# One PSUM tile for the grouped products, and score buffers of a bank and a half in the attention

## The chip, the cores and the metric

The kernel runs on one core of one Trainium2 chip. The metric is the device time of one execution in microseconds (us), the median of several runs. A core has a matrix engine (TensorE, PE in the profile, with its weight loads shown apart as PEld), a vector engine (VectorE, DVE), a scalar engine (ScalarE, ACT), a general engine (GpSimd, POOL) and a queue engine (SyncE, SP). Each takes its instructions in order. Matrix products land in PSUM, 128 partitions of eight banks; a bank holds 512 fp32 numbers of a partition. From there DVE or ACT read them.

## The reference, cut to what matters

One layer of a block with two parallel mixers over 512 latent tokens of width 2048. A combined projection gives queries, keys, values, gates and the input of a Fourier mixer. Twelve query heads share four key and value heads; the keys are the 512 tokens and 256 context tokens, so each block of 128 queries meets 768 keys:

```
s = jnp.einsum('bqhgd,bkhd->bhgqk', qi, k, preferred_element_type=jnp.float32)
w = jax.nn.softmax(s, axis=-1).astype(v.dtype)
return jnp.einsum('bhgqk,bkhd->bqhgd', w, v)
...
y_a = (attn * jax.nn.silu(z_a)) @ w_pa
y_b = (_fourier_mix(u_b) * jax.nn.silu(z_b)) @ w_pb
return (g_a * y_a + g_b * y_b) @ w_o
```

All is fp32. The kernel gets fp32 accuracy from three products of split operands.

## The kernel before, in words

**Split products.** `mm3` (lines 292 to 296) computes one product of two operands that are each held as a high and a low part: high by high (L294), high by low (L295) and low by high (L296). `split_from` (L161) makes the parts: ACT writes the high part (L162), then DVE writes the low part (L163).

**Stages.** First come the modulation and the start of the projection, with a PSUM pool of their own that is closed at L655. Then the groups of 1024 output columns (`KINDS`, L58: three of queries and gates "qz", two gates, one "kv", two gates), then the attention, then the projection of both branches, merged, and the output product as two more groups.

**Groups.** A group is computed by seven products of half-size blocks (`ONE_GROUP`, L52; a Strassen form), each of 48 matrix instructions. P1 and P2 sum up in the PSUM buffer "a", Q5, Q6 and Q3 in "b", P7 and Q4 in "c". "a" and "c" are pairs of banks under the name "x", "b" under the name "y". After each product the sum is taken out by ACT or DVE (L756 to L782); after Q4 the DVE subtraction of `sub` (L756) reads "c". `qz_done` (L849) takes further pairs as scratch for tanh and rotation. So a qz group takes three pairs of x: for P1, for P7, and for the tanh after P7.

**PSUM before.** From L662 on one pool `psp` holds two buffers of two banks under the tag x, and one each under y0 and y1. `pair("x")` asks the pool for the next x; the pool decides which of the two it is. `pair("y")` takes turns by hand.

**The attention** (L1109 to L1212) has 48 steps, one for each head and block of 128 queries. In a step, `scores` writes 768 scores into an x pair (matrix instructions of 512 and of 256 columns), DVE takes the maximum (L1118), ACT the exponential (L1120). A step later `turn` transposes the 768 probabilities on PE into `tp`, one of the y pairs (six instructions, L1136), and `split_from` makes them into high and low (`pth`, `ptl`). Every other step `values` multiplies them with the values in half of the other y pair (18 instructions of 256 columns) and transposes the gate (L1151). `turn_queries` transposes the next head's queries (L1017), `get_keys` the next keys (L1010). `filler` (L1076) puts products of the Fourier branch in between, into the other half of that y pair; ACT copies them out (L1096).

**Order.** The program is written in the order above, but a scheduler of the framework orders the instructions of each engine anew and sets the semaphores. It keeps two engines out of one PSUM bank: an instruction that writes a bank waits until the readers of that bank are done, also where they read other columns of it. What depends on what is kept per tile: a new tile of the pool waits for the whole old one. Weights come by DMA on SP's queue (L198, L201), sums of weights by accumulating DMA on POOL's (L250).

Of the kernel before, what the change touches and what calls it, by code (L numbers as in the profile page):

```python
# [10 lines left out]
F32 = mybir.dt.float32  # L11
# [7 lines left out]
P = 128  # L19
# [8 lines left out]
NKEY = T + C  # L28
# [79 lines left out]
def block_kernel(ctx, tc, xT, ctx_rows, ctx_toks, x, c_row, w_ss, w_gate, vecs, qkg, rope, dft_c, dft_s,  # L108
# [29 lines left out]
    def uid(s):  # L138
        cnt[0] += 1
        return f"{s}{cnt[0]}"  # L140
# [20 lines left out]
    def split_from(src, hi, lo):  # L161
        nc.scalar.activation(hi, src, ACT.Copy)  # L162
        return nc.vector.tensor_tensor(lo, src, hi.bitcast(F32), op=ALU.subtract)  # L163
# [92 lines left out]
    def get(key):  # L256
        load_more()
        turn = [e for e in ahead if not e.aside]
        assert turn[0].key == key, (turn[0].key, key)
        for e in turn[: len(hl_pools)]:  # L260
            split_piece(e)
        load_more()
        e = turn[0]
        ahead.remove(e)
        free.extend(p[0::2] for p, _ in e.raws if p in retired)
        return e.raws[0][1] if e.kind == "raw" else e.out
# [15 lines left out]
    def take(shape, dt=F32, pool=None):  # L282
        p = next((p for p in free if p[0] is pool), free[0])
        free.remove(p)
        t = slot_tile(p, shape, dt)
        home[id(t)] = p, t
        return t

    def give(*ts):
        free.extend(home.pop(id(t))[0] for t in ts)  # L290

    def mm3(o, ah, al, bh, bl, start, stop, cont=False):

        nc.tensor.matmul(o, ah, bh, start=start, stop=False, skip_group_check=cont)  # L294
        nc.tensor.matmul(o, ah, bl, start=False, stop=False, skip_group_check=cont)  # L295
        nc.tensor.matmul(o, al, bh, start=False, stop=stop, skip_group_check=cont)  # L296
# [34 lines left out]
    def tiles(key):  # L331

        new = [take((1024,), F32R) for _ in range(2)]
        kept.setdefault(key, []).extend(new)
        return new
# [15 lines left out]
    flat = lambda v: v.rearrange("p t c -> p (t c)")  # L351
# [14 lines left out]
    for g in range(LAST + 1):  # L366
        for name in ONE_GROUP:
            if (g, name) == (LAST, "Q4"):
                stream_keys(0)
            if g == KV:  # L370
                f = CTX_FORMS.index(next(f for n, f, _, _ in PRODUCTS if n == name))
# [288 lines left out]
    new_ev = lambda: evp.tile([P, 2, 512], F32, tag="ev", bufs=4, name=uid("ev"))  # L660
    qzs, qzp = region("qzp", "right", reuse_waits="tile")
    psp = ctx.enter_context(tc.tile_pool(name="psp", bufs=1, space=PSUM, reuse_waits="tile"))  # L662
    last_y = [0]
    rows4 = lambda hi, lo: [(hi[:, j, :], lo[:, j, :]) for j in range(4)]

    def make_form(f, h):
# [20 lines left out]
        return rows4(hi, lo)  # L687

    def pair(tag, skip=0):
        if tag == "y":  # L690
            last_y[0] += 1 + skip
            return psp.tile([P, 2, 512], F32, tag=f"y{last_y[0] % 2}", bufs=1, name=uid(tag))
        return psp.tile([P, 2, 512], F32, tag=tag, bufs=2, name=uid(tag))


    forms = {"A11": [(hhi[j][:, :256], hlo[j][:, :256]) for j in range(8)],
# [9 lines left out]
    class Banks:  # L706


        def __init__(self):
            self.b = [pair("x") for _ in range(2)]  # L710
# [4 lines left out]
    class Group:  # L715
# [12 lines left out]
        def run(self, name):  # L728
            form, which = next((f, c) for n, f, _, c in PRODUCTS if n == name)
            start = which not in self.acc  # L730
            if start:

                self.acc[which] = Banks() if self.last and which == "c" else pair(self.tags[which])
# [137 lines left out]
    class Context:  # L871
# [13 lines left out]
        def products(self, name, which, pc, w, start):  # L885
            a = self.acc[:, 1 if which == "b" else 0, :]
            for k in range(2):
                j = 2 * pc + k
                fh, fl = (f.parts[j // 4][:, j % 4 // 2, P * (j % 2) : P * (j % 2) + P] for f in self.f)
                mm3(a, fh, fl, w[0][:, k, :], w[1][:, k, :], start and pc == 0 and k == 0, pc == 3 and k == 1,  # L890
                    cont=not start)
# [23 lines left out]
        def values(self, b, v):  # L915
            nc.scalar.dma_start(by_group(v_d[:, :, 4 + b, :]), v.rearrange("p (g d) -> p g d", g=4))
# [60 lines left out]
    def load_row(half):  # L977
        row = crow[half] = take((1024,)) if half else rp.tile([P, 1024], F32, tag="raw1", bufs=1, name=uid("crow"))
        nc.gpsimd.dma_start(row, c_row[:, 1024 * half : 1024 * half + 1024].broadcast_to([P, 1024]))

    def silu_of_row(half):

        e, row = take((1024,)), crow[half]
        nc.scalar.activation(e, row, ACT.Tanh, scale=0.5)
        nc.vector.scalar_tensor_tensor(row, e, 1.0, row, op0=ALU.add, op1=ALU.mult)
        give(e)
# [15 lines left out]
    def load_head(h):  # L1002
        qz[h] = take((2, 4, HD))
        nc.gpsimd.dma_start(qz[h], qz_d[h])

    def get_keys(g):
        raw = get(("K", g))
        tk = flat(pair("x"))
        for t in range(KT):
            nc.tensor.transpose(tk[:, t * P : (t + 1) * P], raw[:, t * P : (t + 1) * P], ident)  # L1010
        keys = tiles(g)
        split_from(tk[:, :NKEY], *(w[:, :NKEY] for w in keys))
        kv[g] = tuple(keys) + get(("V", g))

    def turn_queries(h, tq):
        for t in range(4):
            nc.tensor.transpose(tq[:, t * P : (t + 1) * P], qz[h][:, 0, t, :], ident)  # L1017
        qs[h] = take((2, T), F32R)
        split_from(tq, qs[h][:, 0, :], qs[h][:, 1, :])
# [47 lines left out]
    free += [(hm, f"s{(9 + i) % KK}") for i in range(KK)]  # L1067
    ats_, atp = region("atp", "right", reuse_waits="tile")

    turned_y = last_y[0] % 2  # L1070
    both = pair("y")
    fill_acc, b1 = both[:, 0, :], lambda: both[:, 1, :]
    assert not any(p[0] is gvp or p[2] == "raw1" for e in ahead for p, _ in e.raws)
    ybs, S = {}, {}

# [26 lines left out]
    def fill(n):  # L1102
        for _ in range(n):
            next(fl, None)
# [4 lines left out]
    def scores(i):  # L1109
        h, t = divmod(i, 4)  # L1110
        kh, kl = kv[h // GQ][:2]
        s = slice(t * P, (t + 1) * P)
        qh, ql = qs[h][:, 0, s], qs[h][:, 1, s]
        sc = flat(pair("x"))
        for a, b in ((0, 512), (512, 768)):
            mm3(sc[:, a:b], qh, ql, kh[:, a:b], kl[:, a:b], True, True)
        mx = stats[:, 4 * (i % 4) : 4 * (i % 4) + 4]
        nc.vector.tensor_reduce(mx[:, 0:1], sc[:, :NKEY], axis=AX.X, op=ALU.max, negate=True)  # L1118
        probs[i] = take((NKEY,))
        nc.scalar.activation(probs[i], sc[:, :NKEY], ACT.Exp, bias=mx[:, 0:1], accum_out=mx[:, 1:2])  # L1120
        if t == 3:
            give(qs.pop(h))

    def divide(i):

        h, t = divmod(i, 4)
        z = qz[h][:, 1, t, :]
        r = stats[:, 4 * (i % 4) + 2 : 4 * (i % 4) + 3]
        nc.vector.reciprocal(r, stats[:, 4 * (i % 4) + 1 : 4 * (i % 4) + 2])
        nc.vector.tensor_scalar(z, z, r, None, op0=ALU.mult)  # L1130

    def turn(i):
        p = probs.pop(i)
        tp = flat(psp.tile([P, 2, 512], F32, tag=f"y{turned_y}", bufs=1, name=uid("tp")))
        for k in range(KT):
            nc.tensor.transpose(tp[:, k * P : (k + 1) * P], p[:, k * P : (k + 1) * P], ident)  # L1136
        if i % 2 == 0:
            pts[i // 2] = [atp.tile([P, KT, 256], F32R, tag=n, bufs=2, name=uid(n)) for n in ("pth", "ptl")]
        c = slice((i % 2) * P, (i % 2) * P + P)
        split_from(tp[:, :NKEY].rearrange("p (k q) -> p k q", k=KT), *(w[:, :, c] for w in pts[i // 2]))  # L1140
        give(p)
# [38 lines left out]
    for i in range(NSTEP + 3):  # L1180
        h, t = divmod(i, 4)
        if i < NSTEP:
            if t == 1 and h + 2 < NH:
                load_head(h + 2)
            if i == 24:
                load_row(0)
            elif i == 28:
                silu_of_row(0)
            if i % 12 == 10 and i // 12 + 1 < NKV:
                get_keys(i // 12 + 1)  # L1190
            scores(i)
        want = min(3 + 61 * (i + 1) // NSTEP, 64)
        if want > filled:
            fill(1)
            filled += 1
        if i % 2 == 0 and i >= 4:
            values((i - 4) // 2)
        if 1 <= i <= NSTEP:
            turn(i - 1)
            divide(i - 1)  # L1200
        if t == 1 and h + 1 < NH:
            turn_queries(h + 1, b1())
        if want > filled:
            fill(want - filled)
            filled = want
        if i == NSTEP - 1:
            fill(1)
            first_sums = [pair("x") for _ in range(2)]
            first = products(CHUNKS[0], first_sums)
        if NSTEP > i - 2 >= NSTEP - 3:  # L1210
            next(first)
            next(first)  # L1212
# [12 lines left out]
    m = -1  # L1225
# [46 lines left out]
    for n, j in enumerate(CHUNKS):  # L1272
# [9 lines left out]
        for pc, t in products(j, accs) if n else first:  # L1282
# [4 lines left out]
            if pc > 3:  # L1287
                y = ybs[j, pc - 4]
# [274 lines left out]
```

## Time and profile before

| | |
|---|---|
| median of 3 runs | 1337.47 us (1337.39 to 1337.62) |
| the profiled execution | 1337.45 us |
| its span in the profile | 1335.7 us |
| granted PE clock | 0.998 |
| PE busy | 1299.3 us, 97% of the span |
| DVE busy | 978.5 us, 73% |
| ACT busy | 653.9 us, 49% |
| POOL busy | 138.1 us, 10% |
| HBM read | 263.37 MB |

The span runs from the first to the last instruction of the program; the 1.75 us between it and the execution's time lie around it. PE is the busiest engine and the durations of its instructions overlap, so "busy" is not the same as "at its peak". The attention with the filler takes the stretch from about 815 us to 1030 us.

### The profile page before, as it was taken

To read this page: it belongs to the slowest core of one execution; us is meant where nothing else is said; L and a number is where in the kernel's file an instruction comes from. 1 tells how busy PE (TensorE), PEld (TensorE's weight loads), DVE (VectorE), ACT (ScalarE), POOL (GpSimd) and SP (SyncE) were. 2 spreads that over 40 slices of the span, in tenths; PEclk is the share of its full clock that TensorE was granted. 3 is DMA by queue.
4 is the path that set the end of the run, shared out by engine and by line. 5 is a ranking of instruction groups with operands and counts; after the bars stand their busy time and mean duration, and the time that the engine had idled before them with its cause. 6 is when DMAs were issued, how large, how long until landed. Compare 5 with 4: busy or idle time off the path is not lost. (4 is left out here: it accounts for less than half of the span.)

```text
span 1335.7 us, 17491 instructions
## 1 busy us (share of the span) xinstructions
PE 1299.3 (97%) x6594; PEld 1061.3 (79%) x6594; DVE 978.5 (73%) x1287; ACT 653.9 (49%) x1018; POOL 138.1 (10%) x186
## 2 busy tenths in 40 slices
PE   6999999999999999999999999999999999999996
PEld 3566888888888887888887888788888888878884
DVE  4655989877778868646477666677776789777677
ACT  5322655555555545444264455666665223464544
POOL 1110011110301011011021110000000100111210
PEclk9999999999999999999999999999999999999999
DMA  9996677887897999777679786122113989778974
GB/s 383 393 380 251 222 193 205 220 223 221 204 313 191 299 268 279 246 164 181 189 188 310 207 240 224 33 68 79 48 48 111 334 319 337 189 159 236 225 201 142
DMA packets 96085, 291.28 MB, mean 218 GB/s; under 512 B 8960, under 2 KB 32000, under 8 KB 91648
## 3 DMA queue, kind: packets, MB, share of 16 engines
q1 hardware_dynamic: 51600, 172.95, 37.3%
q0 software_dynamic: 21936, 94.39, 29.0%
q10 hardware_dynamic: 22464, 22.81, 5.1%
q8 instruction: 52, 0.85, 0.2%
q14 instruction: 33, 0.27, 0.1%
HBM read 263.37 MB, written 26.75 MB: 217 GB/s over the span
## 5 line engine op out<-in xcount | busy, mean ns | idle before, releaser
L162 ACT ACTIVATE whi<-wr 128x1024 fp32r<-128x1024 f32 (+1 forms) x129 | 135.6, 1052 | 195.6 <-PE y L296 87.4
L294 PE MATMUL y<-whi,s 128*128 128x512 f32 x544 | 214.9, 395 | 1.1 <-ACT s L762 1.1
L295 PE MATMUL x<-wlo,s 128*128 128x512 f32 x548 | 213.8, 390 | 1.2 <-DVE wlo L163 1.2
L294 PE MATMUL x<-whi,s 128*128 128x512 f32 x548 | 214.1, 391 | 0.2 <-ACT s L759 0.2
L295 PE MATMUL y<-wlo,s 128*128 128x512 f32 x544 | 212.4, 390 | 1.1 <-DVE wlo L163 1.1
L296 PE MATMUL x<-whi,s 128*128 128x512 f32 x548 | 213.3, 389 | 0.0
L296 PE MATMUL y<-whi,s 128*128 128x512 f32 x544 | 211.9, 390 | 0.0
L163 DVE TENSOR_TENSOR wlo<-wr,whi 128x1024 fp32r<-128x1024 f32 (+1 forms) x129 | 156.0, 1213 | 62.4 <-ACT whi L162 62.4
L162 ACT ACTIVATE whi<-R 128x1024 fp32r<-128x1024 f32 x115 | 121.3, 1059 | 127.8 <-PE x L296 58.5
L163 DVE TENSOR_TENSOR wlo<-R,whi 128x1024 fp32r<-128x1024 f32 x115 | 139.9, 1222 | 50.4 <-ACT whi L162 50.4
L294 PEld LDWEIGHTS y<-whi,s 128*128 128x128 f32 x544 | 102.1, 188 | 24.8 <-DVE s L1160 2.3
L295 PEld LDWEIGHTS x<-wlo,s 128*128 128x128 f32 x548 | 102.9, 188 | 23.3 <-DVE wlo L163 2.4
L294 PEld LDWEIGHTS x<-whi,s 128*128 128x128 f32 x548 | 102.9, 188 | 21.9 <-ACT s L759 0.5
L296 PEld LDWEIGHTS x<-whi,s 128*128 128x128 f32 x548 | 102.8, 188 | 21.5
L296 PEld LDWEIGHTS y<-whi,s 128*128 128x128 f32 x544 | 102.1, 188 | 21.6
L295 PEld LDWEIGHTS y<-wlo,s 128*128 128x128 f32 x544 | 102.2, 188 | 20.5 <-DVE wlo L163 1.5
L294 PE MATMUL x<-s,s 128*128 128x512 f32 (+1 forms) x274 | 104.5, 381 | 4.2 <-ACT s L1120 3.1
L295 PE MATMUL x<-s,s 128*128 128x512 f32 (+1 forms) x284 | 106.6, 375 | 0.0
L296 PE MATMUL x<-s,s 128*128 128x512 f32 (+1 forms) x284 | 106.1, 374 | 0.0
L250 POOL DMA_DIRECT2D R<-in_w_g x64 | 55.4, 866 | 425.2 <-DVE wlo L163 314.6
L162 ACT ACTIVATE s<-wr 128x512 fp32r<-128x512 f32 (+2 forms) x94 | 61.8, 674 | 55.8 <-PE y L295 16.3
L163 DVE TENSOR_TENSOR s<-wr,s 128x512 fp32r<-128x512 f32 (+2 forms) x94 | 67.6, 743 | 22.4 <-ACT s L162 20.6
(275 smaller groups left out, 2257.3 us busy)
## 6 DMA issues: line engine op xcount, KB each, us to landing
wr<-in_w_g SPq DMA_DIRECT2D x128, 512.0 KB, 4.9
R<-in_w_g POOLq DMA_DIRECT2D x64, 512.0 KB, 6.6
wa<-in_w_ss POOLq DMA_DIRECT2D x28, 1024.0 KB, 9.0
R<-in_w_g SPq DMA_DIRECT2D x32, 512.0 KB, 5.1
wr<-in_w_pab SPq DMA_DIRECT2D x32, 512.0 KB, 4.7
wr<-in_w_gate SPq DMA_DIRECT2D x32, 512.0 KB, 5.4
wr<-in_w_o SPq DMA_DIRECT2D x24, 512.0 KB, 6.6
R<-in_w_o POOLq DMA_DIRECT2D x24, 512.0 KB, 7.3
```

Source lines behind the costliest of these rows:

```text
L162: nc.scalar.activation(hi, src, ACT.Copy)
L163: return nc.vector.tensor_tensor(lo, src, hi.bitcast(F32), op=ALU.subtract)
L250: nc.gpsimd.dma_start(chain[e.pc], e.nxt, accum_op=ALU.add)
L294: nc.tensor.matmul(o, ah, bh, start=start, stop=False, skip_group_check=cont)
L295: nc.tensor.matmul(o, ah, bl, start=False, stop=False, skip_group_check=cont)
L296: nc.tensor.matmul(o, al, bh, start=False, stop=stop, skip_group_check=cont)
```

## The change

All eight banks become one tile, `banks`, and the program says itself which part of it each use gets. In the groups `pair` counts the uses of x and of y and hands out pairs of banks in strict turn: x is banks 2 and 3, then 0 and 1, and so on; y is 6 and 7, then 4 and 5. In the attention the first six banks are cut into four buffers of 768 columns, a bank and a half each (`wide`): `wide[0]` is bank 0 and half of bank 1, `wide[1]` the other half of bank 1 and bank 2, `wide[2]` bank 3 and half of bank 4, `wide[3]` the other half of bank 4 and bank 5. The scores, and the later keys, take turns with the first three; the transposed probabilities have `wide[3]`. Bank 6 is the filler's, bank 7 that of values and queries. Where a buffer starts in the middle of a bank the scores are written as 256 and 512 columns instead of 512 and 256.

```
+    banks = psp.tile([P, 8, 512], F32, name="banks")
+    given = {"x": 0, "y": 0}
...
     def pair(tag, skip=0):
-        if tag == "y":
-            last_y[0] += 1 + skip
-            return psp.tile([P, 2, 512], F32, tag=f"y{last_y[0] % 2}", bufs=1, name=uid(tag))
-        return psp.tile([P, 2, 512], F32, tag=tag, bufs=2, name=uid(tag))
+        given[tag] += 1 + skip
+        b = 2 * (given[tag] % 2) + (4 if tag == "y" else 0)
+        return banks[:, b : b + 2, :]
...
+    turn_wide = [0]
+
+    def next_wide():
+        turn_wide[0] += 1
+        return wide[turn_wide[0] % 3]
+
     def get_keys(g):
         raw = get(("K", g))
-        tk = flat(pair("x"))
+        tk = next_wide() if g else flat(pair("x"))
...
-    turned_y = last_y[0] % 2
-    both = pair("y")
-    fill_acc, b1 = both[:, 0, :], lambda: both[:, 1, :]
+    wide = [flat(banks)[:, NKEY * i : NKEY * i + NKEY] for i in range(4)]
+    fill_acc, b1 = banks[:, 6, :], lambda: banks[:, 7, :]
...
-        sc = flat(pair("x"))
-        for a, b in ((0, 512), (512, 768)):
+        sc = next_wide()
+        m = 512 if sc is not wide[1] else 256
+        for a, b in ((0, m), (m, NKEY)):
             mm3(sc[:, a:b], qh, ql, kh[:, a:b], kl[:, a:b], True, True)
...
-        tp = flat(psp.tile([P, 2, 512], F32, tag=f"y{turned_y}", bufs=1, name=uid("tp")))
+        tp = wide[3]
...
-            first_sums = [pair("x") for _ in range(2)]
+            first_sums = [banks[:, 2 * b : 2 * b + 2, :] for b in range(2)]
```

More of the change, by code (lines that the diff above doesn't have):

```diff
@@ L662, in block_kernel @@
     psp = ctx.enter_context(tc.tile_pool(name="psp", bufs=1, space=PSUM, reuse_waits="tile"))
-    last_y = [0]
+    banks = psp.tile([P, 8, 512], F32, name="banks")
+    given = {"x": 0, "y": 0}
     rows4 = lambda hi, lo: [(hi[:, j, :], lo[:, j, :]) for j in range(4)]
```

## The prediction, made before the changed kernel was run

> **What bounds the kernel now.** I read the engine totals first, then the attention's stretch alone, then who waited for whom in it. The totals:
>
> ```profile
> span 1335.7 us, 17491 instructions
> PE 1299.3 (97%) x6594; PEld 1061.3 (79%) x6594; DVE 978.5 (73%) x1287; ACT 653.9 (49%) x1018; POOL 138.1 (10%) x186
> ```
>
> PE sets the time. What does not shorten PE's work or its gaps changes nothing, and a gap on PE costs its full length. The change adds and removes no instruction: PE, DVE, ACT, POOL and SP issue as many as before, the DMAs among them; a dozen DMAs stand two or three places elsewhere in their queues. So the whole effect is gaps. In the attention's stretch, 815 to 1030 us (columns: length, then busy time of PE, PEld, DVE, ACT, POOL):
>
> ```profile
> 815.00:1030.00 215.00, 209.32 (x1363) 183.45 (x1361) 153.64 (x259) 132.52 (x229) 5.81 (x11) 1.00 0.24 79
> ```
>
> PE is idle for 215.00 - 209.32 = 5.7 us. That is nearly all that the attention can give. Whom PE waited for there, and below it the same for the weight loads, which feel a wait first (columns: us in total, times, longest):
>
> ```profile
> PE x L294 <- ACT s L1120: 3.1, 5, 1.1
> PE x L294 <- ACT s L162: 1.1, 1, 1.1
> ...
> PE x L1010 <- ACT s L1120: 0.6, 1, 0.6
> PE tp L1136 <- DVE ptl L163: 0.3, 1, 0.3
> ```
> ```profile
> PEld x L294 <- ACT s L1120: 4.4, 5, 1.3
> PEld tp L1136 <- DVE ptl L163: 2.7, 9, 0.8
> ...
> PEld x L1010 <- ACT s L1120: 0.8, 1, 0.8
> ```
>
> So the two score buffers do bind: five times the scores, and once the keys, waited for the exponential that empties the buffer. The single `tp` buffer hardly binds. What such a wait consists of:
>
> ```profile
> L1118 DVE TENSOR_REDUCE gain<-x 128x1 f32<-128x768 f32 x48 | 45.4, 951 | 3.6 <-PE x L296 3.4
> L163 DVE TENSOR_TENSOR ptl<-tp,pth 128x768 fp32r<-128x768 f32 x47 | 44.9, 956 | 16.7 <-ACT pth L162 16.4
> L1120 ACT ACTIVATE s<-x,gain 128x768 f32<-128x768 f32 x48 | 43.2, 901 | 22.6 <-DVE gain L1118 19.9 <-DVE gain L1129 1.7 <-PE y L296 0.9
> ...
> L162 ACT ACTIVATE pth<-tp 128x768 fp32r<-128x768 f32 x48 | 38.9, 811 | 18.7 <-PE tp L1136 18.3
> ```
>
> A score buffer is free one maximum and one exponential after its last product: 0.951 + 0.901, with handovers about 2.2 us. `tp` is free one ACT and one DVE split after its last transposition: 0.811 + 0.956, with handovers about 2.0 us. PE moves on meanwhile; its instructions follow each other at the distance of their starts:
>
> ```profile
> 880.36 0.28 PE L294 MATMUL x<-s,s 128*128 128x256 f32 x1
> 880.47 0.28 PE L295 MATMUL x<-s,s 128*128 128x256 f32 x1
> ...
> 880.71 0.40 PE L294 MATMUL y<-whi,s 128*128 128x512 f32 x1
> 880.94 0.40 PE L295 MATMUL y<-wlo,s 128*128 128x512 f32 x1
> ```
>
> 0.23 us for 512 columns, 0.12 for 256. A transposition takes about 0.11.
>
> **Part 1: strict turns in the groups.** A qz group takes three x pairs, an odd number: P1, P7, tanh. With strict turns the next group's P1 gets the pair in which Q4 has just been summed. Before, the pool gave it the other pair, as the boundary of the first two groups shows (Q4's last product starts at 250.53, P1 at 250.75, both named x; DVE takes Q4's sum out afterwards):
>
> ```profile
> 250.53 0.39 PE L296 MATMUL x<-whi,s 128*128 128x512 f32 x1
> 250.75 0.39 PE L294 MATMUL x<-whi,s 128*128 128x512 f32 x1
> ...
> 251.10 1.22 DVE L756 TENSOR_TENSOR ev<-x,ev 128x1024 f32<-128x1024 f32 x1
> ```
>
> Now P1 has to wait for L756: until 251.10 + 1.22 + 0.1 = 252.4 instead of 250.75, 1.67 us later. Behind it stands all of PE's work. The changed kernel's order puts products of Q5 into the gap: two at the boundaries of the groups 0/1 and 2/3 (326.8 and 404.9 are the other two places of L756), eight at 1/2. Two give back 2 x 0.23 = 0.46, eight 1.84. Net 1.2 us twice and nothing once: **+2.4 us**. The two need their weights' high part, which ACT writes only after Q4's last product:
>
> ```profile
> L162 ACT ACTIVATE whi<-wr 128x1024 fp32r<-128x1024 f32 (+1 forms) x129 | 135.6, 1052 | 195.6 <-PE y L296 87.4
> ```
>
> 250.75 + 0.1 + 1.05 + 0.46 = 252.4, no later than L756. Bounds: nothing, if P1 finds the bank free after all; and 2 x 1.2 + 2 x 1.22 = 4.9 if another DVE instruction of L756's length stands ahead of it each time. The gates and kv have an even or harmless sequence, and the order after the attention is the same instruction for instruction.
>
> **Part 2: the third score buffer.** The waits above go: by PE's own rows 3.1 + 0.6 = 3.7 us, by the loads' 4.4 + 0.8 = 5.2. I take PE's, **-3.7**. What is late next stands in part 3.
>
> **Part 3: the shared banks.** `wide[0]` and `wide[1]` share bank 1, `wide[2]` and the transposed probabilities share bank 4. No buffer before shared a bank with another of its kind, so no row prices it. The waits in the changed kernel's order show what happens: the third of `wide[1]` in bank 1 waits for the exponential of `wide[0]` and the reverse, the third of `wide[2]` in bank 4 waits for the splits of the last `tp`, and the two transpositions in bank 4 wait for the exponential of `wide[2]`. The other two thirds are free earlier, and the order makes use of it: it writes the free bank first and puts other products before the rest. But the buffers are not three.
>
> I count how tight this is: for each PE wait of the attention, the PE work (by the distances above) between the product that starts the chain and the instruction that waits, less the chain of 2.2 or 2.0 us. Waits on an exponential with less than 1 us to spare: 13 before, most with 0.64 to spare; 20 after, 12 of them with under 0.3. Waits on the two splits: 28 before, 42 after. Of the 13, six stalled and cost 3.7, 0.28 each; of the 28 the loss was 0.3 to 2.7, 0.01 to 0.1 each. At the same rates the new order pays 20 x 0.28 = 5.6 and 42 x 0.01 = 0.5: **+5.6 + 0.2**. By the loads' rows it is -5.2 + 8.0 + 1.4 = +4.2 net instead of +2.1. The lower bound is that the order hides the new waits wholly (0); the upper that each of the 20 stalls as long as the mean of the six by the loads, 5.2/6 = 0.87: 17.
>
> The rates are the weakest step. ACT and DVE take their queues in order, and a wait stalls when something else stands before the exponential. Such a case before:
>
> ```profile
> 882.69 0.81 ACT L162 ACTIVATE pth<-tp 128x768 fp32r<-128x768 f32 x1 [0.50 <-PE tp L1136]
> ...
> 883.40 0.90 ACT L1120 ACTIVATE s<-x,gain 128x768 f32<-128x768 f32 x1
> ...
> 884.44 0.50 PE L294 MATMUL x<-s,s 128*128 128x512 f32 x1 [0.59 <-ACT s L1120]
> ```
>
> The exponential stood behind a split that itself waited for PE. In the changed order the same two kinds of ACT work, and the query splits, alternate as closely.
>
> A rule speaks against this change: the Trainium skill, "PSUM — Partial Sum Buffer", section "PSUM bank collisions raise a hardware error", tells authors to guard PSUM by bank and not by address, since two engines must not be in one bank at once. By it the gain of 3.7 would shrink to that of a buffer whose last third is not free, the 1340 us of the second rival. No run here shows a collision.
>
> **Sum.** The profiled execution took 1337.45 us, its span 1335.7 and 1.75 around it; the median is 1337.47, so the same sum serves both. 1337.45 + 2.4 - 3.7 + 5.6 + 0.2 = 1341.95, **1342 us**, 0.34% slower. Writing 256 columns ahead of 512 costs nothing: the same instructions. What can be told from no change in this kernel is about 0.2%, 2.7 us: faster is below 1334.8, slower above 1340.1.
>
> **Rivals.**
> (a) Faster: the new waits are covered, since two thirds of each buffer are written early. The point that decides is whether the exponentials of `wide[2]` come before PE reaches the two transpositions in bank 4. For it: DVE and ACT are idle 29% and 38% of the stretch. Against: 12 of the 20 have nothing to spare. 1337.45 - 3.7 (or 5.2) with 0 to 2.4 for the boundaries and a remainder of 0.5 of small waits: 1332.8 to 1336.6, likeliest 1335.
> (b) It does not do what it says: the shared third makes three buffers as good as two, the waits only move. Then part 1 alone remains: 1337.45 + 0 to 2.4 = 1337.5 to 1339.9; by the rule above likewise.
> (c) Bank 4 becomes a loop of its own. Between two turns of `wide[2]` it carries three times two transpositions with their splits and one score third with its exponential: 3 x (0.22 + 2.0) + 0.35 + 2.2 = 9.2 us. The turns themselves show how long three steps take:
>
> ```profile
> L1136 PE MATMUL tp<-ident,s x288: 270/272/331, 831.8 to 1029.6; 128*128 128x128 f32 x144
> ```
>
> (1029.6 - 831.8)/47 = 4.2 us a step, 12.6 for three. The loop binds when its four handovers are late by more than 3.4 us together; with the 0.87 of the stalled waits each it is just covered. Half a us more of each is 16 x 2 = 32 at worst; I put 8 to 14 on it: 1346 to 1352.
>
> **How the numbers follow.** Forecast 0.50 (1340.3 to 1346; it includes the loads' rates, 1344), (a) 0.19, (b) 0.22, (c) 0.09. Faster by over 0.2%: of (a) what lies below 1334.8, and a little more if the queries' wait of 1.1 also goes: 0.16. Within: the rest of (a), nearly all of (b), a little of the forecast: 0.27. Slower: 0.57. For 8 in 10 the range leaves out the lower half of (a) and the upper half of (c): **1334.5 to 1348**. The forecast's own range is 1340.1 to 1346.
>
> **What would show it.** Part 1: at two of the three boundaries (about 251 and 405 us, 327 spared) a PE wait of about 1.2 us on DVE L756. Wrong if P1 follows Q4 without a gap. Part 2: no PE wait on L1120 by scores that write a bank of their own. Part 3: PE waits on L1120 by L1136, and of score thirds on L163, 5 to 6 us together, and the attention's stretch about 2 us longer; PE's idle time in it about 7.8 us instead of 5.7. If the stretch is 3 us shorter, (a) holds; if DVE and ACT are seldom idle before the splits while PE waits at each third step, (c). The forecast fails if the queue order of ACT and DVE in the changed kernel, which a count of distances does not see, is kinder or worse than before.

## The result and the profile after

The changed kernel takes 1344.15 us (median of 6 runs, 1342.18 to 1346.9) against 1337.25 of before (6 runs, 1335.25 to 1337.62): a ratio of 1.006, 95% interval 1.0048 to 1.0071, so 0.6% slower. The forecast was 1342, in the range 1334.5 to 1348. The direction is right and the size close, but the trace shows that this is luck: errors of 5 to 7 us cancel. The profiled execution took 1342.18 us. Its totals, read as those of before:

```profile
span 1340.4 us, 17479 instructions
PE 1304.2 (97%) x6594; PEld 1061.9 (79%) x6594; DVE 980.6 (73%) x1287; ACT 652.3 (49%) x1018; POOL 134.1 (10%) x186
```

PE is busy 4.9 us longer with the same 6594 instructions, and the mean granted clock is 0.995 instead of 0.998: already a hint that some of the loss is no wait. Where it was lost follows from the start of PE's n-th instruction in both traces (differences worked out from the rows of all 6594):

| PE's n-th instruction | in before at, us | changed minus before, us |
|---|---|---|
| 1050, ahead of the groups | 167.0 | -1.0 |
| 1200 | 195.5 | +0.1 |
| 1500 | 264.1 | +1.4 |
| 2100 | 400.1 | +1.8 |
| 2250 | 434.1 | +7.5 |
| 3300 | 674.1 | +6.9 |
| 3450 | 709.7 | +11.3 |
| 3900, end of the groups | 811.7 | +11.3 |
| 5250, end of the attention | 1026.9 | +6.5 |
| 6593 | 1324.8 | +4.7 |

So the groups lose 12 us and the attention gains 5. The forecast had the groups lose 2.4 and the attention 2.1.

**The groups.** Whom PE waited for between 170 and 815 us, first before, then after (columns as in the prediction: us in total, times, longest):

```profile
PE y L295 <- DVE s L163: 2.0, 1, 2.0
PE y L295 <- DVE wlo L163: 1.1, 1, 1.1
PE y L296 <- DVE s L163: 0.3, 1, 0.3
```
```profile
PE banks L295 <- DVE wlo L163: 3.9, 3, 1.9
PE banks L294 <- DVE ev L757: 2.5, 2, 2.3
PE banks L294 <- ACT whi L162: 2.4, 2, 1.2
PE banks L295 <- DVE s L163: 1.0, 1, 1.0
PE banks L294 <- DVE part L633: 0.8, 1, 0.8
```

Four kinds are new or longer. Two of them, L757 (L756 of before) and the weights' high part ahead of it, are the strict turns. The timeline of the changed kernel at the worst boundary, 405 us:

```profile
403.73 1.23 DVE L239 TENSOR_TENSOR R<-R,wr 128x1024 f32<-128x1024 f32 x1
403.95 0.39 PE L296 MATMUL banks<-whi,s 128*128 128x512 f32 x1
404.43 1.06 ACT L162 ACTIVATE whi<-R 128x1024 fp32r<-128x1024 f32 x1 [1.05 <-PE banks L296]
404.87 1.22 DVE L163 TENSOR_TENSOR wlo<-R,whi 128x1024 fp32r<-128x1024 f32 x1
...
405.54 0.73 PE L294 MATMUL banks<-whi,s 128*128 128x512 f32 x2 [1.21 <-ACT whi L162]
406.12 1.22 DVE L239 TENSOR_TENSOR R<-R,wr 128x1024 f32<-128x1024 f32 x1
407.26 1.22 DVE L757 TENSOR_TENSOR ev<-banks,ev 128x1024 f32<-128x1024 f32 x1
...
408.53 0.50 PE L294 MATMUL banks<-s 128*128 128x512 f32 x1 [2.26 <-DVE ev L757]
```

Q4's last product starts at 403.95. The two products of Q5 that were put into the gap wait for their weights until 405.54. P1 waits for L757, and ahead of L757 DVE first splits and adds further weights (L163, L239), so P1 starts at 408.53. From Q4's last product to P1 three products' distances would have done: 408.53 - 403.95 - 3 x 0.23 = 3.9 us are lost. At 251 us no such pair stands ahead, only the rest of one L239, and 251.82 - 249.30 - 0.69 = 1.8 us are lost:

```profile
249.30 0.39 PE L296 MATMUL banks<-whi,s 128*128 128x512 f32 x1
249.41 1.22 DVE L239 TENSOR_TENSOR R<-R,wr 128x1024 f32<-128x1024 f32 x1
...
250.55 1.22 DVE L757 TENSOR_TENSOR ev<-banks,ev 128x1024 f32<-128x1024 f32 x1
...
250.88 0.73 PE L294 MATMUL banks<-whi,s 128*128 128x512 f32 x2 [1.20 <-ACT whi L162]
...
251.82 0.50 PE L294 MATMUL banks<-whi,s 128*128 128x512 f32 x1 [0.20 <-DVE ev L757]
```

What follows at 410 us is no wait. PE's instructions of 512 columns follow each other at 0.43 us instead of 0.23:

```profile
410.43 0.63 PE L295 MATMUL banks<-s,s 128*128 128x512 f32 x1
410.85 0.63 PE L296 MATMUL banks<-s,s 128*128 128x512 f32 x1
411.28 0.63 PE L294 MATMUL banks<-s,s 128*128 128x512 f32 x1
```

The view by stretches gives the granted clock in the column after POOL's busy time. It is 0.66 in the 5 us after this wait, and again after a wait at 716 us:

```profile
405.00:409.00 4.00, 1.20 (x4) 0.72 (x5) 3.97 (x4) 0.98 (x4) 0.00 (x0) 1.00 0.70 205
409.00:414.00 5.00, 5.00 (x17) 3.95 (x16) 5.00 (x10) 3.12 (x16) 3.13 (x3) 0.66 0.72 158
...
716.00:721.00 5.00, 5.00 (x16) 3.91 (x16) 5.00 (x6) 1.06 (x1) 2.16 (x3) 0.66 0.89 176
```

(1 - 0.66) x 5 = 1.7 us each time, lost while PE shows as busy. The third kind, `wlo`, is longer at 690 and 716 us, behind the kv group. After, then before, the same place in DVE's queue (lines of other engines left out):

```profile
684.97 1.21 DVE L845 TENSOR_TENSOR qr<-qr,banks 128x1024 f32<-128x1024 f32 x1
...
686.70 0.69 DVE L927 TENSOR_TENSOR cxe<-cxe,small 128x512 f32<-128x512 f32 x1 [0.52 <-POOL small L827]
...
687.31 1.22 DVE L846 TENSOR_TENSOR qr<-qr,small 128x1024 f32<-128x1024 f32 x1
...
688.45 2.35 DVE L163 TENSOR_TENSOR wlo<-R,whi 128x1024 fp32r<-128x1024 f32 x2
...
689.72 0.50 PE L295 MATMUL banks<-wlo,s 128*128 128x512 f32 x1 [1.76 <-DVE wlo L163]
```
```profile
678.08 0.69 DVE L926 TENSOR_TENSOR cxe<-cxe,small 128x512 f32<-128x512 f32 x1 [0.59 <-POOL small L826]
...
678.69 2.35 DVE L163 TENSOR_TENSOR wlo<-R,whi 128x1024 fp32r<-128x1024 f32 x2
...
681.56 0.43 DVE L841 TENSOR_TENSOR y<-ev,qr 128x256 f32<-128x256 f32 x1
```

After, the rotation of the keys (L842 to L846; L841 to L845 of before) is done before the weights' split that PE waits for; before, it came behind it. The fourth kind, `part`, is the first product of the groups, which now waits for the last reader of the PSUM pool ahead.

**The attention.** The answer to the prediction's row of its stretch, and whom PE and then the weight loads waited for in it:

```profile
826.00:1037.00 211.00, 209.81 (x1367) 182.61 (x1366) 154.28 (x259) 132.52 (x229) 5.81 (x11) 1.00 0.25 82
```
```profile
PE banks L294 <- ACT pth L162: 0.6, 1, 0.6
PE banks L294 <- ACT s L162: 0.5, 1, 0.5
```
```profile
PEld banks L1145 <- DVE ptl L163: 3.4, 12, 0.4
PEld banks L1145 <- ACT s L1129: 2.1, 9, 0.3
...
PEld banks L294 <- ACT s L1129: 1.0, 3, 0.4
PEld banks L294 <- DVE ptl L163: 0.7, 3, 0.3
```

The stretch is 211 us instead of 215, with 1.2 us of idle PE instead of 5.7. The waits of part 3 are there, transpositions on the exponential (L1129) and score thirds on the split of `ptl`, but none is longer than 0.4 us. The question was then whether the third score buffer did this, and what in the groups costs 12.

### The profile page after: what moved, and what is told of

It reads as the page before. It is cut to its first block, busy times and chain, and to the rows that moved or that the text cites. A ratio compares the mean times of both kernels' runs of the same rounds, so it can differ in the third digit from the quotient of the medians.

```text
span 1340.4 us, 17479 instructions
## 1 busy us (share of the span) xinstructions
PE 1304.2 (97%) x6594; PEld 1061.9 (79%) x6594; DVE 980.6 (73%) x1287; ACT 652.3 (49%) x1018; POOL 134.1 (10%) x186
## 4 chain that ended last, share of the span: by engine, by line
PE 84%; DMA 6%; DVE 5%; ACT 3%; issue 2%; POOL 0%; ACTq 0%; SPq 0%; DVEq 0%; POOLq 0%
PE banks L295 23%; PE banks L294 23%; PE banks L296 23%; PE banks L1145 2%; PE pd L482 2%; DMA wr<-in_w_g 2%; DVE wlo L163 2%; PE pb L295 2%; PE pb L294 1%; PE pb L296 1%; DMA wr<-in_w_start 1%; PE pc L294 1%; PE pc L296 1%; PE pc L295 1%; DMA cf_d<-qr 1%
## 5 line engine op out<-in xcount | busy, mean ns | idle before, releaser
L294 PE MATMUL banks<-whi,s 128*128 128x512 f32 x1092 | 427.8, 393 | 4.7 <-ACT whi L162 2.4
L295 PE MATMUL banks<-wlo,s 128*128 128x512 f32 x1092 | 427.5, 391 | 3.9 <-DVE wlo L163 3.9
L296 PE MATMUL banks<-whi,s 128*128 128x512 f32 x1092 | 426.4, 390 | 0.0
L294 PEld LDWEIGHTS banks<-whi,s 128*128 128x128 f32 x1092 | 205.3, 188 | 48.8 <-ACT whi L162 3.2
L295 PEld LDWEIGHTS banks<-wlo,s 128*128 128x128 f32 x1092 | 205.4, 188 | 47.2 <-DVE wlo L163 6.0
L296 PEld LDWEIGHTS banks<-whi,s 128*128 128x128 f32 x1092 | 205.4, 188 | 42.4
L163 DVE TENSOR_TENSOR wlo<-wr,whi 128x1024 fp32r<-128x1024 f32 (+1 forms) x129 | 155.9, 1213 | 60.5 <-ACT whi L162 59.8
L163 DVE TENSOR_TENSOR wlo<-R,whi 128x1024 fp32r<-128x1024 f32 x115 | 140.1, 1221 | 55.7 <-ACT whi L162 55.5
L295 PE MATMUL banks<-s,s 128*128 128x512 f32 (+1 forms) x436 | 166.5, 382 | 1.1 <-DVE s L163 1.0
L294 PE MATMUL banks<-s,s 128*128 128x512 f32 (+1 forms) x426 | 164.8, 388 | 0.5 <-ACT s L162 0.5
L296 PE MATMUL banks<-s,s 128*128 128x512 f32 (+1 forms) x436 | 164.8, 381 | 0.0
L295 PEld LDWEIGHTS banks<-s,s 128*128 128x128 f32 x436 | 82.4, 189 | 17.0 <-DVE s L163 1.9
L294 PEld LDWEIGHTS banks<-s,s 128*128 128x128 f32 x426 | 80.3, 189 | 18.6 <-ACT s L162 1.1
L296 PEld LDWEIGHTS banks<-s,s 128*128 128x128 f32 x436 | 82.0, 189 | 15.2
L163 DVE TENSOR_TENSOR s<-wr,s 128x512 fp32r<-128x512 f32 (+2 forms) x94 | 67.9, 742 | 31.6 <-ACT s L162 31.2
L162 ACT ACTIVATE s<-R 128x512 fp32r<-128x512 f32 (+1 forms) x83 | 54.3, 666 | 40.2 <-PE banks L296 28.1
L241 DVE TENSOR_TENSOR wr<-R,wr 128x1024 f32<-128x1024 f32 x40 | 48.7, 1221 | 33.9 <-DMA wr<-in_w_g 21.2
L163 DVE TENSOR_TENSOR s<-R,s 128x512 fp32r<-128x512 f32 (+1 forms) x83 | 59.1, 730 | 13.3 <-ACT s L162 13.2
```

The costliest lines, as they stand in the source:

```text
L241: nc.vector.tensor_tensor(src, chain[e.pc], src, op=ALU.subtract)
```

## The experiments

Each was timed in rounds together with the kernel of before (1336.7 to 1337.3 there). "Attention" is the time from the first transposition of keys to the last of probabilities: 814.9 to 1029.6, 214.7 us, in before, whose row of the probabilities stands in the prediction (the range of start times stands behind the durations) and whose row of the keys is:

```profile
L1010 PE MATMUL x<-ident,wr x24: 270/272/328, 814.9 to 965.0; 128*128 128x128 f32 x24
```

In the changed kernel the first row is the keys' and the second that of the probabilities:

```profile
L1017 PE MATMUL banks<-ident,wr x24: 270/272/328, 826.1 to 974.7; 128*128 128x128 f32 x24
```
```profile
L1145 PE MATMUL banks<-ident,s x288: 270/273/330, 844.1 to 1036.5; 128*128 128x128 f32 x144
```

1036.5 - 826.1 = 210.4 us.

**a1, the attention's part alone.** The pool of before until the last group, then closed, and the one tile from there on:

```
+    pso.close()
+    psb = ctx.enter_context(tc.tile_pool(name="psb", bufs=1, space=PSUM, reuse_waits="tile"))
+    banks = psb.tile([P, 8, 512], F32, name="banks")
     wide = [flat(banks)[:, NKEY * i : NKEY * i + NKEY] for i in range(4)]
```

> The groups keep the pool of before (two tags of pairs, the pool chooses), the pool is closed at the end of the last group, and the one tile with its four buffers of a bank and a half begins with the attention; PE's order up to the attention is that of before, instruction for instruction. Theory G (the groups lose, the attention gains; from the two traces: up to the attention's first transposition of keys the changed kernel is 11.3 us behind, at the last transposition of probabilities about 6.3): 1337.3 - 5.0 = 1332.3, between 1331 and 1334, PE idle or late in the attention about 5 us less than before. Theory F (the forecast on record: groups +2.4, attention 5.6 + 0.2 - 3.7 = +2.1): 1339.4. A new wait at the place where the pool is closed could add 1 to 2 to either.

Measured: 1331.86 us, ratio 0.9964 (0.9952 to 0.9976). Theory F is out. The attention part alone is a gain of 5.2 us, even with a new wait of 1.5 where the pool is closed.

**a2, the groups' part alone.** One tile and strict turns; the attention cut as before, on that tile:

```
-        sc = next_wide()
+        sc = flat(pair("x"))
-        tp = wide[3]
+        tp = turned_y
```

> The one tile and the strict turns from the groups on, but in the attention the pairs of banks of before: two score buffers of two banks in turn, the transposed probabilities in a pair of their own, filler and values in the last pair. Theory G: 1337.3 + 11 = 1348, between 1345 and 1351, with PE waits of 1.7 us at 251, of 3.8 at 405 followed by some 3.5 us at half clock, and of about 2 at 690 and 716. Theory F: 1337.3 + 2.4 = 1339.7.

Measured: 1343.77 us, ratio 1.0047 (1.0031 to 1.0064). Slower, but 4 us less than theory G says. The waits stand where it put them (by PE's starts, beyond the usual 0.23: 1.35 and 0.37 at 253, 1.36 and 2.70 at 407 and 410, 1.93 at 692, 2.13 at 718, with half the clock after the one at 410). What it missed is the attention: laid out as before, with two score buffers, it took 826.5 to 1033.3, 206.9 us. That is 7.9 less than before and 3.5 less than with three buffers. So the third buffer was not the cause of the gain. By the whole time a2 is only 0.7 us ahead of the changed kernel in the same rounds (a4 below), less than the noise.

**a3, one turn skipped.** The changed kernel, with the next P1 sent to the other pair:

```
             e = pair("x" if half else "y")
+            given["x"] += half
```

> The changed kernel with one turn of x skipped after each tanh pair in a qz group, so that the next group's P1 gets the pair that Q4 does not hold, as the pool chose before; all else as changed. If the three boundaries of the qz groups cost what the trace shows there (1.7 + 0.4 + 5.7 = 7.8, the half clock included): 1344.2 - 7.8 = 1336.4, and the waits on L757 are gone. By the forecast (+2.4 for them): 1341.8. If the boundary waits come from the single tile and not from the turns: 1344, no change.

Measured: 1337.99 us, ratio 1.0007 (0.9998 to 1.0016), 6.2 to 6.5 less than the changed kernel. The waits on L757 are gone, and with them the ones on `whi`. The forecast's price of the turns is out. The waits at 174, 690 and 716 stay (the last two at 686 and 713 there).

**a4, the changed kernel again.**

> The changed kernel once more, beside the three others on the same chip: 1342 to 1347, as before. If the waits at 690 and 716 and the half clock after 408 and 716 belong to this kernel, this profile shows them again at the same places; if they are chance of one execution (a late DMA), they stand elsewhere or are gone.

Measured: 1344.47 us, ratio 1.006 (1.0048 to 1.0072). Waits again at 174, 253, 408 and 693 us, that at 693 now 3.5 us long and followed by half the clock, that at 719 shorter (0.6). The places belong to the kernel; how long the last two are, and which wait is followed by half the clock, differs from execution to execution.

**b1, the old layout on one tile, from the attention on.** a1 with two score buffers of two banks, the transposed probabilities in a pair, filler and values in the last pair:

```
-    wide = [flat(banks)[:, NKEY * i : NKEY * i + NKEY] for i in range(4)]
-    fill_acc, b1 = banks[:, 6, :], lambda: banks[:, 7, :]
+    four += [banks[:, 2 * i : 2 * i + 2, :] for i in range(4)]
+    turned_y = flat(four[2 + given["y"] % 2])
+    both = pair("y")
+    fill_acc, b1 = both[:, 0, :], lambda: both[:, 1, :]
```

> Groups with the pool of before; from the attention on one tile of eight banks, but cut as before: two score buffers of two banks in turn, the transposed probabilities in a pair, filler and values in the two banks of the last pair. Theory T (the attention gains by the single tile, in which a write waits only for readers of its own bank, while in a tile of two banks it waits for the readers of both; the third score buffer is not the cause): 1337.1 - 7.9 = 1329.2 as in the attention of the run with the groups alone, up to 1330.7 with the wait of 1.5 where the pool is closed. Theory B (the third score buffer is the cause, as the forecast's part 2 has it): no gain, 1337.

Measured: 1330.41 us, ratio 0.9954 (0.9938 to 0.9969): theory T, with the wait of 1.5 at the seam; theory B is out. It beats both kernels.

**b2, three things in one tile of four banks.** b1 with other tiles:

```
-    banks = psb.tile([P, 8, 512], F32, name="banks")
-    four += [banks[:, 2 * i : 2 * i + 2, :] for i in range(4)]
+    half = psb.tile([P, 4, 512], F32, name="half")
+    four += [psb.tile([P, 2, 512], F32, name=f"pair{i}") for i in range(2)]
+    four += [half[:, 2 * i : 2 * i + 2, :] for i in range(2)]
```

> As the run before, but the attention's PSUM in three tiles: two of two banks for the scores, and one of four banks for the transposed probabilities, the filler and the values. Nothing else differs. Theory T: in the tile of four banks each filler product waits for the splits of the transposed probabilities and each transposition for the readers of the values; of the 48 steps each loses 0.5 to 1 us: 1361 to 1385. Theory B: the buffers and their number are those of before, so 1337, as before.

Measured: 1476.67 us, ratio 1.1042 (1.1024 to 1.106). The mechanism is that of theory T, the size far beyond it. PE's waits in b2's attention, and a stretch of it with about as many PE instructions as that of before (1345 against 1363):

```profile
PE half L294 <- DVE ptl L163: 36.0, 24, 2.0
PE half L1026 <- DVE ptl L163: 20.1, 11, 2.0
PE half L1152 <- DVE s L1176: 10.0, 11, 1.4
```
```profile
815.00:1168.00 353.00, 259.65 (x1345) 212.79 (x1344) 151.61 (x256) 133.16 (x224) 5.17 (x10) 0.86 0.14 44
```

Fillers (the 24 waits of L294 are all `half<-whi`) and the queries' transpositions (L1026) wait for the split of the transposed probabilities, which reads two other banks; the transpositions of the probabilities (L1152) wait for the readers of the values (L1176). By bank none of these touch. PE is idle 353.0 - 259.7 = 93.3 us instead of 5.7, and the granted clock of 0.86 takes another 0.14 x 353 = 49: together 137 of the 138 by which the stretch is longer. The expectation had 24 to 48 for the waits, which took 93.3 - 5.7 = 87.6 more, and had left out the clock.

**b3, the strict turns alone.** Four tiles of two banks, taken once and handed out in strict turn; the attention as before:

```
-    banks = psp.tile([P, 8, 512], F32, name="banks")
+    four = [psp.tile([P, 2, 512], F32, name=f"pair{i}") for i in range(4)]
-        return banks[:, b : b + 2, :]
+        return four[given[tag] % 2 + (2 if tag == "y" else 0)]
```

> The strict turns alone: four tiles of two banks, taken once and handed out in strict turn from the groups on, and the attention laid out as before. By the forecast's part 1 (two boundaries of 1.2): 1337.1 + 2.4 = 1339.5. By the changed kernel's trace (1.7 at 251, 0.4 at 328, 3.8 at 405, and 1.9 more if half the clock follows the long wait): 1343 to 1345; the waits at 174, 690 and 716 then are absent, if they belong to the single tile. If the turns cost nothing by themselves: 1337.

Measured: 1344.66 us (1339.85 to 1346.91), ratio 1.0063 (1.005 to 1.0077). The turns alone cost as much as the whole change. PE's waits from 170 to 815 us in b3:

```profile
PE pair L294 <- ACT whi L162: 2.4, 2, 1.2
PE pair L295 <- DVE wlo L163: 1.3, 1, 1.3
...
PE pair L294 <- DVE ev L756: 1.2, 2, 0.8
```

No wait on `part`, and one on `wlo` as before: those belong to the single tile. The attention took 213.4 us, nearly that of before: tiles that are taken once do not bring the gain. The profiled execution, the fastest, loses 5.9 in the groups. The runs spread with the clock: 1339.85 at a mean of 0.997, 1346.91 at 0.992; 0.005 x 1340 = 6.7 of the 7.1 between them.

**b4, one tile, the turn skipped, the old layout.** a3 with the attention of a2:

```
-        sc = next_wide()
+        sc = flat(pair("x"))
-        tp = wide[3]
+        tp = turned_y
```

> One tile from the groups on with the skipped turn after tanh, and in the attention the layout of before with two score buffers: it differs from the run with the skipped turn in the attention's layout alone. Theory T (third buffer and shared banks cost 2.9 against two buffers in the one tile): 1338.0 - 2.9 = 1335.1. Theory B (third buffer gains 5): 1343.

Measured: 1335.35 us, ratio 0.9985 (0.997 to 0.9999): theory T. Its attention took 821.6 to 1028.5, 206.9 us. Against a3 the third buffer with its shared banks costs 2.6. By the starts of the same PE instructions it falls behind before from 1.9 us ahead of the groups to 6.8 at 710 us: 4.9 for the single tile in the groups, without the turns. The medians say the same: b4 less b1, which has the groups of before, is 4.9, and a3 less a1 is 6.1. One execution can lose more: a3's profiled one, 2.5 slower than its median, loses 9.7 in the groups, two drops of the clock included.

**c1, the filler apart.** The pool of before until the last group, and the layout of before in the attention, with tiles of two banks taken once; only filler and values have a tile of one bank each.

```
-    both = pair("y")
-    fill_acc, b1 = both[:, 0, :], lambda: both[:, 1, :]
+    fill_acc, values_acc = (psf.tile([P, 512], F32, name=n) for n in ("fillb", "valb"))
+    b1 = lambda: values_acc
```

> Groups with the pool of before, attention laid out as before, two score buffers and the transposed probabilities each in a tile of two banks; the one thing changed is that the filler and the values have a tile of one bank each instead of one tile of two banks. If the false wait between filler and values (a write to one of the two banks waits for the readers of both) is what the single tile took away, this gives the whole gain: 1337.2 - 7 = 1330, as the old layout on one tile, and up to 1.5 less if the wait at the closing of the pool is gone too (1328.7 to 1330.5). If the gain needs the eight-bank tile for the scores or the transposed probabilities as well, less than half of it: 1334 to 1337.

Measured: 1329.81 us, ratio 0.995 (0.9933 to 0.9967): the whole gain, 6.9 us. Against b3, whose pairs are also taken once, the attention differs in the filler's tile and the seam. The attention's waits of PE in c1:

```profile
PE pair L294 <- DVE ev L759: 1.3, 1, 1.3
PE pair L294 <- ACT s L1139: 0.2, 1, 0.2
```

The waits on the exponential (L1139, L1120 before), which the forecast took for the mark of a missing score buffer (3.1 and 0.6 us by PE's rows), are 0.2 with the same two buffers. The wait at the seam, on L759, stays.

**c2, b1 again, beside c1.**

> The old layout on one tile from the attention on, once more, beside the run with the filler apart on the same chip: 1329.4 to 1332.4 as before. The difference of the two is the seam alone, 0 to 1.5.

Measured: 1330.31 us, ratio 0.9955 (0.9938 to 0.9971). It and c1 can't be told apart.

## Why the prediction was right, and where it was wrong

The sum was 1341.95. Put the measured terms in: the turns cost 7.4 (b3 less its before) instead of 2.4, the single tile in the groups 4.9 (b4 less b1) instead of nothing, the attention -5.2 (a1 less its before) instead of +2.1; the wait at the seam, which a1 and b1 both have, cancels. 1341.95 + 5.0 + 4.9 - 7.3 = 1344.55, and 1344.15 was measured. Three terms were off by 5 to 7 us each; the likeliest case held because they cancelled, which is luck.

- **What bounds the kernel.** Right: no engine's instruction came or went (the 12 by which the totals differ are semaphore waits of the sequencers), and the time is lost in PE's gaps and just behind them. But "a gap on PE costs its full length" is too little: a long gap was followed by 1.7 us at reduced clock.
- **Part 1, the strict turns.** The mechanism is right, with its places: P1 waits for L756 (now L757) at two boundaries, the eight products of Q5 cover the third but for 0.4 us. The size failed, at "Now P1 has to wait for L756: until 251.10 + 1.22 + 0.1", which takes over how soon DVE came to L756 in before: 0.57 us after the start of Q4's last product (251.10 - 250.53). In the changed kernel it is 1.25 at 251 (250.55 - 249.30, behind L239) and 3.31 at 405 (407.26 - 403.95, behind L163 and L239). That is 0.7 and 2.7 later, which turns the forecast's 1.2 into the 1.8 and 3.9 above, to within 0.1; the clock's drop adds 1.7. The prediction's upper bound of 4.9 named such an instruction of DVE, but the waits alone came to 1.8 + 0.4 + 3.9 = 6.1. How late DVE comes to the subtraction at 405 is not the same in every trace with the strict turns: 3.6 us in a2, 2.4 in a4, 1.6 in b3. What sets it stays open.
- **"The gates and kv have an even or harmless sequence."** This step failed. The order of turns is harmless there, but the single tile changes what an instruction depends on: DVE's order differs at the end of the kv group, and the first product waits for the last reader of the pool ahead. b3 and a3 separate the two: turns without the single tile lack these waits, the single tile without the turns has them. That the key rotation comes early because its scratch pair is free sooner is argued from DVE's order, not shown; nor is it shown that the wait at 716 follows from the late split at 690 by way of a later transfer.
- **Part 2, "So the two score buffers do bind."** Failed. The waits were real, but c1 removes them with two buffers. In before, filler and values lie in one tile of two banks, and there a write to one bank waits for the readers of both; the loads' rows of before show it, in the stretch of the attention, as waits of the filler's products (the rows behind it are all `y<-whi`) on the reader of the values (L1160) and of the queries' transpositions (L1017) on the copy of the filler (L1096):

```profile
PEld y L294 <- DVE s L1160: 2.3, 10, 0.2
...
PEld y L1017 <- ACT s L1096: 0.5, 2, 0.3
```

  These waits are short, but PE's order differs where they are allowed for: in it the scores stand close behind the exponential that frees their buffer. That the scheduler draws the scores forward because the filler must wait is argued; that the order and the waits on the exponential change with the filler's tile alone is shown. Counted as in part 3, waits on the exponential with less than 1 us to spare are 13 before and at most 1 in b1 and c1.
- **Part 3, the rates.** Failed in size and sign of the net. The new waits are there (transpositions on the exponential 2.1 us by the loads' rows, score thirds on the split 0.7), but PE's own rows show none of them. A rate from before's order (0.28 us a tight wait) does not carry over to another order. Against two buffers in a tile tracked by bank, the third with its shared banks costs: 3.5 us by the attention's length (210.4 in the changed kernel, a3 and a4, about 206.9 in a2 and b4), by the whole time 2.6 (a3 against b4), 1.5 (a1 against b1) and 0.7 (a4 against a2), of which only the first is clear of the noise, and barely. How this divides between the shared banks and the less regular order stays open; PE's rows show only about 1 us more of idle time for it.
- **The rivals.** (a) had the attention's direction right, and by the prediction's own sign, a stretch 3 us shorter, it would hold there (it is 4.3 shorter); but its reason, a third buffer that pays, is wrong. (b), made from the turns and a third buffer that is worth nothing, lacked the gain that has nothing to do with buffers. (c), the loop through bank 4, is nowhere to be seen: no wait in the attention is over 0.9 us even by the loads' rows. The rule of the Trainium skill, "PSUM — Partial Sum Buffer", section "PSUM bank collisions raise a hardware error", to guard by bank, agrees with the nine short waits of transpositions on the exponential, but it did not decide the time.

## What to carry to other kernels

Before a buffer is added because PE waits for an emptied one, look for short waits between uses that share nothing but a tile: in this framework a tile of two or four PSUM banks is waited for as a whole, one of a bank or of all eight by banks, and taking the false wait away was worth 0.5% where the extra buffer brought nothing and cost up to 0.2%. A change of allocation can change every engine's order, as it did here, so price the stages it only passes through as well, and read how soon the engine that frees a buffer comes to it in the new order. A gap on PE of over 2 us can bring 1.7 us of reduced clock with it.

## What the runs showed of the hardware

The granted clock falls after waits that are short. In the eleven profiles besides b2's, from 170 us on, a single pause with 2.1 to 2.7 us between the starts of two PE instructions was followed by a stretch at half pace (0.43 us a product of 512 columns instead of 0.23, some 3.4 us long) 3 times in 13; both single pauses of 2.9 us and more were (2.97, for 6.8 us, and 3.70); the double pause at 405 us (1.6 and 1.3 to 2.9, within 5 us) was 4 times in 4; pauses under 2.1 us alone were not. The Trainium skill, "TensorE: Matmul & The Clock Gate", section "HAM oscillation — how this bites in real kernels", advises to keep PE's pauses under about 3.4 us; here the half pace came after less, and the length of the slow stretch fits that figure.
